# Experts: TensorE's work put in the order in which the passes are written

## The chip, the cores and the metric

The kernel runs on one core of one Trainium2 chip. TensorE multiplies matrices into PSUM, VectorE (DVE) and ScalarE (ACT) read PSUM and work on SBUF, GpSimd (POOL) helps with small things, SyncE (SP) issues the loads of the weights. The metric is the device time of one execution in microseconds, as the median of several runs.

## What is computed

The reference is a chain of two blocks of two layers each over 256 tokens of width 1024. The first block has an even mixer (gated delta rule and dilated attention), an odd mixer (differential attention and gated linear attention) and convolutional feed-forwards; the second has stick-breaking attention and retention, each followed by a mixture of experts. The change touches the mixture of experts alone, which runs once in each layer of the second block:

```python
def grouped_moe(h, router_w, router_b, w_gate, w_up, w_down):
    t = h.reshape(B * S, Dm)
    logits = t.astype(jnp.float32) @ router_w.astype(jnp.float32) + router_b.astype(jnp.float32)
    ...
    combine = jnp.sum(jax.nn.one_hot(top_idx, N_EXPERTS, dtype=jnp.float32) * top_w[..., None], axis=1)
    out = jnp.zeros(t.shape, jnp.float32)
    for e in range(N_EXPERTS):
        hidden = jax.nn.silu(t @ w_gate[e]) * (t @ w_up[e])
        out = out + combine[:, e:e + 1] * (hidden @ w_down[e]).astype(jnp.float32)
    return out.astype(h.dtype).reshape(B, S, Dm)
```

There are 16 experts, each with three matrices of 2 MB (1024 x 512 floats); a token uses two of them. 96 MB of weights are read per layer.

## The kernel before

The program is one straight line for one core. The router sorts the tokens to experts. Then `moe` works in nine passes: eight `Pair`s of experts (64 token places for each of two experts, 128 in all) and at last a `Unit`, which gives the last expert of the order 64 more places. Passes for experts that are still fuller (`more`) follow behind branches.

A pass n consists of these steps, by the names of the code:

- gather(n) (`slots`, lines 2067 to 2096): VectorE makes a selection matrix `pe`; TensorE multiplies it with the tokens (L2081, 16 matmuls of 128 columns, into the PSUM banks `ps`), and VectorE and ScalarE bring the result to `xs` (L449, L447). Two small products (L2089, L2091) give the weights `cw` and the transposed selection `pt`.
- gate(n) and up(n) (`up`, L2120): 16 matmuls each of `xs` with pieces of the expert's weights. Those of the pair's two experts alternate; expert e writes partitions 64e to 64e + 63 of the same bank. ScalarE and VectorE form silu of the gate (L728, L729), VectorE the product `h` (L2254).
- flip(n) (L2213): four transposes of `h`, copied to `hT`.
- down(n) (L2131): two halves of 512 columns, the first into the bank `pc`, the second into a bank `ps`, 8 matmuls each, again with the two experts alternating. ScalarE and VectorE weigh the result into `y` (L2099, L2100).
- scatter(n) (L2141): 8 matmuls that add `y` to the four banks of the sum.

The products of gather, gate, up and down are in 32-bit floats, and each of their matmuls shows as two records in the trace. The loop writes them interleaved over the passes: up(n), gather(n+1), scatter(n-1), flip(n), gate(n+1), down(n), and so on. But the order in the program is not that of the code. A planner sorts all instructions by what its own model of the engines says is ready, and keeps only what depends on each other in order; so it may put a matmul of gather into the middle of down. What it has put in a row, the engine then runs in that row. Two things hold an order by hand: `keep_in_program_order` for the scatters among themselves, and the helper `ordered` (line 282), which chains each instruction of an engine that is written inside it to the one before.

Weights come in pieces of 1 MB, four for each matrix of a pair: two halves of the matrix for each of two experts. SyncE asks for them (L357) in the order in which they are used: up(n), gate(n+1), down(n). They go to 20 buffers in three rings (`NW, NQ, NR = 6, 8, 6`), and a load waits until the piece that held its buffer is used up. Behind the last of them SyncE has the first weights of the next stage. The number of passes behind branches is read into a register of each engine at L2278.

Of the kernel before, what the change touches and what calls it, by code (L numbers as in the profile page):

```python
# [10 lines left out]
F32 = mybir.dt.float32  # L11
# [5 lines left out]
ALU = mybir.AluOpType  # L17
# [4 lines left out]
P = 128  # L22
S = 256
NT = S // P
D = 1024
KD = D // P
# [92 lines left out]
class Net:  # L119
# [1862 lines left out]
    def moe(self, layer, xn, out=None):  # L1982
        nc, T, tc = self.nc, self.T, self.tc
        tt, stt, ts = nc.vector.tensor_tensor, nc.vector.scalar_tensor_tensor, nc.vector.tensor_scalar
        mm = nc.tensor.matmul
        ia = 2 * layer + 1
        scale, shift = self.adac[:, ia, 8:16], self.adac[:, ia, :8]
# [4 lines left out]
        NP = N_EXP // 2  # L1992
        with self.wqs, tc.tile_pool(name=self.nm("wr"), bufs=NR) as self.wr, \
# [5 lines left out]
            def part(e, m, a):  # L1999

                d, n = dram[m], (512, 512, 256)[m]
                v = d[bass.ds(e, 1), a * n : a * n + n, :]
                return v.rearrange("o (k p) f -> p (o k) f", p=P)

            def ask(pr, m, e, a):
                nonlocal nload
                step, w = (4, 4, 2)[m], (wg, wu, wd)[m]
                if pr < 2:
                    src = w[2 * pr + e][:, a * step : a * step + step, :]
                else:  # L2010
                    src = ("dynamic", layer, m, 2 * pr + e, a)
                i = self.wload(src, [P, step, w.shape[3]],
                               ring=("wq" if nload % NB < NQ else "w" if nload % NB < NQ + NW else "wr"))
                pieces.setdefault((pr, m), []).append(i)
                nload += 1

            order = [(0, 0)]
            for pr in range(NP):
                order += [(pr, 1), *([(pr + 1, 0)] if pr < NP - 1 else []), (pr, 2)]
            def ask_all(groups):  # L2020
                for pr, m in groups:
                    for a in range(2):
                        for e in range(2):
                            ask(pr, m, e, a)
# [5 lines left out]
            def big(tag, shape, dt=F32, bufs=1):  # L2030
                if shared is not None and tag in shared:
                    return shared[tag]
                t = mp.tile(shape, dt, tag=tag, name=self.nm(tag), bufs=bufs)
                if shared is not None:
                    shared[tag] = t
                return t


            hT = big("y", [P, KD, S])
            for t in range(NT):  # L2040
                for b in range(0, KD, 4):
                    ps = self.bank()
# [5 lines left out]
            slot, comb, cnt = self.router(mp, hT)  # L2048
            io = cst["iota64"]
            acc = self.newacc()  # L2050
            extra, regs = {}, {}

            def expert_at(n, i):
                if (n, i) not in regs:
                    regs[n, i] = nc.values_load(extra[n][:1, i : i + 1], engines=[mybir.EngineType.SP],
                                                min_val=0, max_val=N_EXP - 1)
                return regs[n, i]

            def by_order():
                for i in range(4, N_EXP):  # L2060
                    for m in range(3):
                        for a in range(2):
                            self.dyn["dynamic", layer, m, i, a] = lambda i=i, m=m, a=a: part(expert_at("pxi", i), m, a)

            fin = list(cols)
# [36 lines left out]
            class Pair:  # L2102

                n = 512
# [40 lines left out]
            class Unit(Pair):  # L2145


                n = 256
# [54 lines left out]
            def gate(it, xs, ps):  # L2203
                ps = it.up(0, xs, ps)
                h = big("h", [P, 512])[:, : it.n]
                self.silu2(h, ps, h)
                return h

            def flip(h):
                n = h.shape[1]  # L2210
                ps = self.bank()
                for f in range(n // P):
                    nc.tensor.transpose(ps[:, f * P : f * P + P], h[:, f * P : f * P + P], self.ident)  # L2213
                hT = big("hT", [P, 512])[:, :n]
                self.copy(hT, ps[:, :n])
                return hT
# [21 lines left out]
                        more(u + 1)  # L2238

            its = [Pair(pr) for pr in range(NP)] + [Unit()]  # L2240
            cur = its[0].slots()
            last = self.last_expert(mp, cnt, slot, comb)
            extra.update(zip(("oh", "pxi", "x", "so", "cb"), last))
            by_order()
            ask_all(order[5:])
            h = gate(its[0], cur[0], self.cb("x"))
            back = None
            for n, it in enumerate(its):
                last = n == NP
                xs, pt, cw = cur  # L2250
                ps = it.up(1, xs, self.cb("x") if n else self.bank())
                if n == NP - 2:
                    extra["m"], extra["off"], extra["exi"] = self.extra_units(mp, extra["x"], extra["oh"])
                tt(h, h, ps, op=ALU.mult)  # L2254
                if not last:
                    cur = its[n + 1].slots()
                if n == 0:
                    for hf in range(2):
                        self.ln_fix(big("xs", [P, KD, P], bufs=2).rearrange("p (m a) c -> p m (a c)", m=2),
                                    xn, 1, layer, 0, hf * 512, 512)  # L2260
                    fin[:] = scale, shift
                if n > 0:
                    back[0].scatter(*back[1:], **({"first": True} if n == 1 else {}))
                hT = flip(h)
                if not last:
                    h = gate(its[n + 1], cur[0], self.bank())
                else:
                    tail, grow = (self.wq.tile([P, 2048], F32, tag="w", name=self.nm("tail")) for _ in range(2))
                    tail = tail.rearrange("p (t c) -> p t c", t=NT)
                    self.ada_gate_to(grow, ia)  # L2270
                back = it, pt, it.down(hT, cw)
            if out is not None:
                gb = self.wr.tile([P, 2048], F32, tag="w", name=self.nm("gb")).rearrange("p (m c) -> p m c", m=2)
                gb = [gb[:, m, :] for m in range(2)]
# [84 lines left out]
```

## Time and profile before

| | us |
|---|---|
| median of 3 runs | 1894.0 |
| lowest, highest | 1893.7, 1896.0 |
| profiled execution, its own time | 1896.7 |
| profiled execution, span from first to last instruction | 1894.7 |

| stage (us from the span's start) | from | to |
|---|---|---|
| experts of the first layer, gate(0) to the last scatter | 1072.6 | 1337.6 |
| retention, up to the experts of the second layer | 1350.5 | 1615.0 |
| experts of the second layer, gate(0) to the last scatter | 1615.0 | 1874.5 |
| last layer norm and output | 1874 | 1894.7 |

The mean granted clock of TensorE over the span is 0.959 of 2.4 GHz. A row of the timeline merges instructions of one line that follow each other: start, duration, engine, line, operation, what it writes and reads, tile, count, and in brackets the idle time before it and what ended that. "128*64" is the part of the array that a matmul uses. A row's duration holds the end of its last matmul, which overlaps the next row's start, so the length of a step is taken from start to start. A row of the windows gives the stretch and its length, the busy time (and count) of TensorE, its weight loads, VectorE, ScalarE and GpSimd, then the granted clock, the mean busy share of the 16 DMA engines and what they moved in GB/s.

### The profile page before, as it was taken

Reading aid. Unit: us, or ns where it says so; the run is one execution under the profiler, and the core shown is the slowest. Engines: PE = TensorE matmul, PEld = TensorE weight load, DVE = VectorE, ACT = ScalarE, POOL = GpSimd, SP = SyncE. Lnnn points to the kernel's source line nnn. Section 1 sums busy time; section 2 is a strip of 40 time slices with the busy share of each in tenths; the row PEclk is TensorE's granted clock in tenths of the full one; section 3 lists DMA queues with packets and bytes.
Section 4 is the critical chain, followed back from the end, with each engine's and each line's share of the span. In section 5 each row is a group of like instructions: output and inputs, shape, how many; then the busy total and the mean of one; then the engine's idle time right before and its main releaser. Section 6 shows DMA issues by size and latency. Waiting matters only on the chain. (4 is left out here: it accounts for less than half of the span.)

```text
span 1894.7 us, 29642 instructions
## 1 busy us (share of the span) xinstructions
PE 1755.2 (93%) x11781; PEld 1348.1 (71%) x11781; DVE 1042.5 (55%) x2003; ACT 711.0 (38%) x1346; POOL 229.7 (12%) x275
## 2 busy tenths in 40 slices
PE   7999998999989989999799799999689997999995
PEld 6989876999879769998798444434589975444432
DVE  6865755877767558777655532111576656422113
ACT  5344434555555445554654111101334332111111
POOL 2111101000043110000300000000133320100002
PEclk9999998999989989999899799999789998999998
DMA  8454544456566674555535899992444458899940
GB/s 271 156 167 157 172 162 158 168 187 201 182 201 210 227 241 156 200 192 183 189 118 202 327 401 399 401 394 68 141 131 154 155 207 329 309 402 399 404 173 24
DMA packets 270059, 422.30 MB, mean 223 GB/s; under 512 B 10357, under 2 KB 175815, under 8 KB 269781
## 3 DMA queue, kind: packets, MB, share of 16 engines
q1 hardware_dynamic: 266516, 415.91, 62.4%
q0 software_dynamic: 2016, 2.49, 0.5%
q8 instruction: 97, 1.59, 0.3%
q10 hardware_dynamic: 1377, 1.88, 0.3%
q14 instruction: 53, 0.43, 0.1%
HBM read 419.19 MB, written 1.05 MB: 222 GB/s over the span
## 5 line engine op out<-in xcount | busy, mean ns | idle before, releaser
L271 DVE TENSOR_TENSOR wl<-w,wh 128x1024 fp32r<-128x1024 f32 (+1 forms) x312 | 386.3, 1239 | 198.5 <-ACT wh L270 194.4
L270 ACT ACTIVATE wh<-w 128x1024 fp32r<-128x1024 f32 (+1 forms) x312 | 328.6, 1055 | 364.1 <-PE ps L404 173.0
L403 PE MATMUL ps<-xh,wh 128*128 128x256 f32 (+1 forms) x1312 | 384.4, 293 | 8.8 <-ACT xh L437 8.0
L404 PE MATMUL ps<-xl,wh 128*128 128x256 f32 (+1 forms) x1312 | 375.9, 287 | 0.0
L405 PE MATMUL ps<-xh,wl 128*128 128x256 f32 (+1 forms) x1312 | 374.9, 286 | 0.1
L403 PEld LDWEIGHTS ps<-xh,wh 128*128 128x128 f32 (+1 forms) x1312 | 252.6, 193 | 16.2 <-ACT xh L437 8.3
L404 PEld LDWEIGHTS ps<-xl,wh 128*128 128x128 f32 (+1 forms) x1312 | 252.6, 192 | 3.2 <-issue 0.8
L405 PEld LDWEIGHTS ps<-xh,wl 128*128 128x128 f32 (+1 forms) x1312 | 252.1, 192 | 2.0 <-issue 0.7
L403 PE MATMUL ps<-wh,xh 128*128 128x256 f32 x512 | 156.5, 306 | 2.5 <-DVE rvg L729 1.9
L405 PE MATMUL ps<-wh,xl 128*128 128x256 f32 x512 | 149.2, 292 | 1.0 <-DVE xl L438 1.0
L404 PE MATMUL ps<-wl,xh 128*128 128x256 f32 x512 | 149.8, 293 | 0.0
L404 PE MATMUL pc<-wl,yh 128*128 128x512 f32 x336 | 132.7, 395 | 0.0
L403 PE MATMUL pc<-wh,yh 128*128 128x512 f32 x336 | 131.7, 395 | 0.9 <-DVE yl L271 0.9
L405 PE MATMUL pc<-wh,yl 128*128 128x512 f32 x336 | 131.2, 391 | 0.3
L2120 PE MATMUL pc<-w,xs 128*64 128x512 f32 x512 | 121.6, 595 | 0.0
L2120 PE MATMUL ps<-w,xs 128*64 128x512 f32 x512 | 113.3, 595 | 0.9 <-ACT pt L265 0.9
L403 PEld LDWEIGHTS ps<-wh,xh 128*128 128x128 f32 x512 | 102.5, 200 | 6.7 <-issue 2.2
L405 PEld LDWEIGHTS ps<-wh,xl 128*128 128x128 f32 x512 | 102.1, 199 | 2.0 <-DVE xl L438 1.8
L404 PEld LDWEIGHTS ps<-wl,xh 128*128 128x128 f32 x512 | 102.7, 201 | 0.4 <-issue 0.2
L2081 PEld LDWEIGHTS ps<-pe,x 128*128 128x128 f32 x576 | 72.3, 204 | 28.1 <-issue 25.2
L2120 PEld LDWEIGHTS pc<-w,xs 128*64 128x64 f32 x512 | 37.4, 137 | 72.8 <-issue 69.8
L2131 PE MATMUL ps<-w,hT 128*64 128x512 f32 x256 | 88.5, 595 | 0.0
(573 smaller groups left out, 2633.3 us busy)
## 6 DMA issues: line engine op xcount, KB each, us to landing
w<-in_moe_w_gate_dram SPq DMA_DIRECT2D x64, 1024.0 KB, 13.2
w<-in_moe_w_up_dram SPq DMA_DIRECT2D x64, 1024.0 KB, 14.6
w<-in_moe_w_down_dram SPq DMA_DIRECT2D x64, 1024.0 KB, 14.2
w<-in_ada_w_dram SPq DMA_DIRECT2D x48, 1024.0 KB, 5.5
w<-in_ffn_w_up_dram SPq DMA_DIRECT2D x44, 1024.0 KB, 5.4
w<-in_ret_w_in_dram SPq DMA_DIRECT2D x24, 1024.0 KB, 5.2
w<-in_ffn_w_down_dram SPq DMA_DIRECT2D x22, 1024.0 KB, 5.1
w<-in_w_in_even_dram SPq DMA_DIRECT2D x21, 1024.0 KB, 5.3
```

Of the source, the lines that this page charges most:

```text
L270: self.nc.scalar.activation(hi, src, AF.Copy)
L271: self.nc.vector.tensor_tensor(lo, src, hi.bitcast(F32), op=ALU.subtract)
L403: mm(ps, lh, rh, start=first, stop=False)
L404: mm(ps, lh, rl, start=False, stop=False)
L405: mm(ps, ll, rh, start=False, stop=last)
L2081: mm(ps[:, k * P : k * P + P], xn[:, t, (4 * a + k) * P : (4 * a + k + 1) * P], pef[:, t, :], start=t == 0, stop=t == 1)
L2120: mm(ps[64 * e : 64 * e + 64, :], xs[:, k, 64 * e : 64 * e + 64], wt[2 * (k // 4) + e][:, k % 4, :], start=k == 0, stop=k == KD - 1)
L2131: mm(ps[64 * e : 64 * e + 64, :], hT[:, f * P + 64 * e : f * P + 64 * e + 64], wt[2 * (f // 2) + e][:, f % 2, hf * 512 : hf * 512 + 512], ...
```

## The change

The nine passes, from the first gather to the ninth pass, are put inside `with self.ordered(nc.tensor.engine)`. Nothing else changes; the body of the loop is the same, indented. The two reads of the router's numbers and the loads that are asked for between the passes stand inside it too, but only instructions of TensorE are chained.

```diff
             its = [Pair(pr) for pr in range(NP)] + [Unit()]
-            cur = its[0].slots()
-            last = self.last_expert(mp, cnt, slot, comb)
...
-            h = gate(its[0], cur[0], self.cb("x"))
-            back = None
-            for n, it in enumerate(its):
...
-                back = it, pt, it.down(hT, cw)
+
+            with self.ordered(nc.tensor.engine):
+                cur = its[0].slots()
+                last = self.last_expert(mp, cnt, slot, comb)
...
+                h = gate(its[0], cur[0], self.cb("x"))
+                back = None
+                for n, it in enumerate(its):
...
+                    back = it, pt, it.down(hT, cw)
```

The helper is the one that the kernel has already:

```python
    def ordered(self, *engines):
        bb = self.nc.cur_bb.bb.instructions
        n = len(bb)
        yield
        last = {}
        for i in list(bb[n:]):
            if i.engine in engines:
                if i.engine in last:
                    self.tc.add_manual_dep(i, last[i.engine], ..., reason="ordered")
                last[i.engine] = i.name
```

In the first layer the rows of TensorE differ from down(3) on, in the second from up(4) on; from there to down(7) they differ in each pass, in the same way. TensorE around down(4) of the first layer, before; `pc_12341` and `ps_12352` are the two halves of down, `w_11635` and `w_11639` pieces of one expert, `w_11637` and `w_11641` of the other, `ps_12387` and `ps_12400` the banks of gather(6):

```order
 L2131 MATMUL pc_12341<-w_11635,hT_12318 64x512
 L2131 MATMUL ps_12352<-w_11635,hT_12318 64x512
 L2081 MATMUL ps_12387<-pe_12384,x_81 128x128 x7
 L2131 MATMUL pc_12341<-w_11637,hT_12318 64x512
 L2131 MATMUL pc_12341<-w_11635,hT_12318 64x512
 L2131 MATMUL pc_12341<-w_11637,hT_12318 64x512
 L2131 MATMUL ps_12352<-w_11637,hT_12318 64x512
 L2131 MATMUL ps_12352<-w_11635,hT_12318 64x512
 L2131 MATMUL ps_12352<-w_11637,hT_12318 64x512
 L2081 MATMUL ps_12387<-pe_12384,x_81 128x128
 L2081 MATMUL ps_12400<-pe_12384,x_81 128x128 x5
```

The same place after the change:

```order
 L2131 MATMUL pc_12341<-w_11635,hT_12318 64x512
 L2131 MATMUL pc_12341<-w_11637,hT_12318 64x512
 L2131 MATMUL pc_12341<-w_11635,hT_12318 64x512
 L2131 MATMUL pc_12341<-w_11637,hT_12318 64x512
 L2131 MATMUL pc_12341<-w_11639,hT_12318 64x512
 L2131 MATMUL pc_12341<-w_11641,hT_12318 64x512
 L2131 MATMUL pc_12341<-w_11639,hT_12318 64x512
 L2131 MATMUL pc_12341<-w_11641,hT_12318 64x512
 L2131 MATMUL ps_12352<-w_11635,hT_12318 64x512
 L2131 MATMUL ps_12352<-w_11637,hT_12318 64x512
```

The first half of down now stands whole ahead of the second, the experts alternate from row to row, and gather(6) has moved behind up(5), where it stands whole ahead of scatter(4).

VectorE's rows follow. From the gate's part of `h` to `hT` of pass 5 in the first layer, before:

```order
 L729 SCALAR_TENSOR_TENSOR h_12337<-h_12337,ps_12320 128x512
 L449 TENSOR_SCALAR xs_12381<-ps_12387,adac 128x128 x2
 L449 TENSOR_SCALAR xs_12381<-ps_12400,adac 128x128
 L2074 TENSOR_TENSOR pe_12533<-cst_9764,upso_11456 128x128 x2
 L449 TENSOR_SCALAR xs_12381<-ps_12400,adac 128x128
 L2100 SCALAR_TENSOR_TENSOR y_12340<-pc_12341,cw_12151,y_12340 128x512
 L2100 SCALAR_TENSOR_TENSOR y_12340<-ps_12352,cw_12151,y_12340 128x512
 L2094 TENSOR_SCALAR cw_12383<-ps_12413 64x1 x2
 L2254 TENSOR_TENSOR h_12337<-h_12337,pc_12363 128x512
 L267 COPY hT_12434<-ps_12429 128x512
```

And after:

```order
 L729 SCALAR_TENSOR_TENSOR h_12337<-h_12337,ps_12320 128x512
 L2100 SCALAR_TENSOR_TENSOR y_12340<-pc_12341,cw_12151,y_12340 128x512
 L2100 SCALAR_TENSOR_TENSOR y_12340<-ps_12352,cw_12151,y_12340 128x512
 L2256 TENSOR_TENSOR h_12337<-h_12337,pc_12363 128x512
 L449 TENSOR_SCALAR xs_12381<-ps_12387,adac 128x128 x2
 L449 TENSOR_SCALAR xs_12381<-ps_12400,adac 128x128
 L2094 TENSOR_SCALAR cw_12383<-ps_12413 64x1 x2
 L2074 TENSOR_TENSOR pe_12533<-cst_9764,upso_11456 128x128 x2
 L449 TENSOR_SCALAR xs_12381<-ps_12400,adac 128x128
 L267 COPY hT_12434<-ps_12429 128x512
```

The weighing of down (L2100) and the product `h` (L2254, now L2256) have moved ahead of what belongs to gather; ScalarE's rows move alike.

SyncE at the end of the first layer's experts, as a difference; `uexi_12520` holds the numbers behind the branches, `w_...` are buffers of the next stage's weights:

```order
 L357 DMA w_11749<-in_ret_w_in_dram 128x8x256
+L2280 TENSOR_LOAD uexi_12520
+L2280 ISA x2
 L357 DMA w_11751<-in_ret_w_in_dram 128x8x256
 L357 DMA w_11753<-in_ret_w_in_dram 128x8x256
 L357 DMA w_11755<-in_ret_w_in_dram 128x8x256
-L2278 TENSOR_LOAD uexi_12520
-L2278 ISA x2
```

The read of the register has moved ahead of three loads. SyncE's loads of the experts' weights keep their order.

## Rows read from the trace of the kernel before

**Rows 1.** The page: the engines' busy time, and a group of down.

```profile
PE 1755.2 (93%) x11781; PEld 1348.1 (71%) x11781; DVE 1042.5 (55%) x2003; ACT 711.0 (38%) x1346; POOL 229.7 (12%) x275
...
L2131 PE MATMUL ps<-w,hT 128*64 128x512 f32 x256 | 88.5, 595 | 0.0
```

**Rows 2.** Windows: first layer, stretches 3 and 6; second layer, stretch 6.

```profile
1146.68:1174.12 27.44, 27.44 (x147) 12.92 (x146) 6.01 (x13) 4.19 (x8) 0.00 (x0) 1.00 1.04 399
1242.96:1277.57 34.61, 33.71 (x148) 13.89 (x147) 5.92 (x13) 4.19 (x8) 0.00 (x0) 1.00 1.03 399
1779.88:1814.49 34.61, 33.72 (x148) 13.89 (x147) 5.92 (x13) 4.18 (x8) 0.00 (x0) 1.00 1.04 397
```

**Rows 3.** Timeline of TensorE, first layer, stretch 3 and the start of 4.

```profile
1146.68 7.09 PE L2120 MATMUL ps<-w,xs 128*64 128x512 f32 x32
1153.60 3.60 PE L2131 MATMUL pc<-w,hT 128*64 128x512 f32 x16
...
1160.46 7.04 PE L2120 MATMUL pc<-w,xs 128*64 128x512 f32 x32
1167.43 3.84 PE L2081 MATMUL ps<-pe,x 128*128 128x128 f32 x32
...
1171.64 2.12 PE L2141 MATMUL pc<-y,pt 128*128 128x512 f32 x8
...
1174.12 7.09 PE L2120 MATMUL ps<-w,xs 128*64 128x512 f32 x32
```

**Rows 4.** Timeline of TensorE, first layer, stretch 6 and the start of 7.

```profile
1249.88 1.02 PE L2131 MATMUL pc<-w,hT 128*64 128x512 f32 x2
...
1265.48 1.35 PE L2141 MATMUL pc<-y,pt 128*128 128x512 f32 x3
...
1276.98 0.66 PE L2213 MATMUL ps<-ident,h 128*128 128x128 f32 x4 [0.78 <-DVE h L2254]
1277.57 7.09 PE L2120 MATMUL ps<-w,xs 128*64 128x512 f32 x32
```

**Rows 5.** SyncE's loads of down(7): durations, first and last issue; issue to landing.

```profile
L357 SPq DMA_DIRECT2D w<-in_moe_w_down_dram x4: 373/704/2358, 1258.6 to 1265.6; - x4
...
DMA to landing us min/median/max: 12.6/13.4/14.2
...
L357 SPq DMA_DIRECT2D w<-in_moe_w_down_dram x4: 1030/1074/2349, 1800.5 to 1805.7; - x4
...
DMA to landing us min/median/max: 13.8/14.5/17.5
```

**Rows 6.** Windows of 10 us, from both layers' stages.

```profile
1100.00:1110.00 10.00, 10.00 (x50) 3.43 (x48) 4.69 (x5) 1.37 (x2) 2.66 (x4) 1.00 1.05 384
...
1280.00:1290.00 10.00, 10.00 (x49) 4.28 (x46) 0.69 (x1) 0.60 (x1) 0.00 (x0) 1.00 0.00 0
...
1340.00:1350.00 10.00, 0.00 (x0) 0.00 (x0) 8.54 (x16) 0.38 (x1) 2.41 (x6) 0.53 0.00 1
...
1620.00:1630.00 10.00, 10.00 (x51) 3.82 (x48) 1.37 (x2) 0.60 (x1) 0.44 (x1) 1.00 0.98 367
```

**Rows 7.** Timeline of TensorE: gate(8) and up(8), gate(4), gate(8) and up(8).

```profile
1312.17 3.67 PE L2178 MATMUL ps<-w,xs 128*64 128x256 f32 x32
...
1323.49 3.67 PE L2178 MATMUL pc<-w,xs 128*64 128x256 f32 x32 [0.72 <-DVE y L2100]
...
1716.63 7.09 PE L2120 MATMUL ps<-w,xs 128*64 128x512 f32 x32
...
1849.09 3.67 PE L2178 MATMUL ps<-w,xs 128*64 128x256 f32 x32
...
1860.41 3.67 PE L2178 MATMUL pc<-w,xs 128*64 128x256 f32 x32 [0.72 <-DVE y L2100]
```

**Rows 8.** Reads of the count at L2278 by GpSimd and by SyncE.

```profile
L2278 POOLq TENSOR_LOAD <-uexi x2: 302/396/491, 1106.1 to 1820.8; - x2
L2278 SPq TENSOR_LOAD <-uexi x2: 267/402/536, 1327.6 to 1809.5; - x2
```

More of the change, by code (lines that the diff above doesn't have):

```diff
@@ L2240, in moe @@
             its = [Pair(pr) for pr in range(NP)] + [Unit()]
-            cur = its[0].slots()
-            last = self.last_expert(mp, cnt, slot, comb)
-            extra.update(zip(("oh", "pxi", "x", "so", "cb"), last))
-            by_order()
-            ask_all(order[5:])
-            h = gate(its[0], cur[0], self.cb("x"))
-            back = None
-            for n, it in enumerate(its):
[L2249 to L2270, printed above, removed]
-                back = it, pt, it.down(hT, cw)
@@ new lines, in moe @@
+            with self.ordered(nc.tensor.engine):
+                cur = its[0].slots()
+                last = self.last_expert(mp, cnt, slot, comb)
+                extra.update(zip(("oh", "pxi", "x", "so", "cb"), last))
+                by_order()
+                ask_all(order[5:])
+                h = gate(its[0], cur[0], self.cb("x"))
+                back = None
+                for n, it in enumerate(its):
+                    last = n == NP
+                    xs, pt, cw = cur
+                    ps = it.up(1, xs, self.cb("x") if n else self.bank())
+                    if n == NP - 2:
+                        extra["m"], extra["off"], extra["exi"] = self.extra_units(mp, extra["x"], extra["oh"])
+                    tt(h, h, ps, op=ALU.mult)
+                    if not last:
+                        cur = its[n + 1].slots()
+                    if n == 0:
+                        for hf in range(2):
+                            self.ln_fix(big("xs", [P, KD, P], bufs=2).rearrange("p (m a) c -> p m (a c)", m=2),
+                                        xn, 1, layer, 0, hf * 512, 512)
+                        fin[:] = scale, shift
+                    if n > 0:
+                        back[0].scatter(*back[1:], **({"first": True} if n == 1 else {}))
+                    hT = flip(h)
+                    if not last:
+                        h = gate(its[n + 1], cur[0], self.bank())
+                    else:
+                        tail, grow = (self.wq.tile([P, 2048], F32, tag="w", name=self.nm("tail")) for _ in range(2))
+                        tail = tail.rearrange("p (t c) -> p t c", t=NT)
+                        self.ada_gate_to(grow, ia)
+                    back = it, pt, it.down(hT, cw)
```

## The prediction

> **What bounds the kernel now.** I read the page first, then the busy time by stretches, then the timeline of the places that the change reorders. TensorE is busy for 93% of the span [rows 1], so what counts is how long its work takes, stage by stage. I count the expert stage in stretches, each from the first matmul of gate(n) to that of gate(n+1): gate(n), down(n-1), up(n), gather(n+1), scatter(n-1), flip(n). A stretch holds the same 147 or 148 matmul records wherever it stands, yet stretch 3 of the first layer takes 27.44 us and stretch 6 takes 34.61, and so does stretch 6 of the second layer. Clock (1.00), DMA rate (397 to 399 GB/s), VectorE's and ScalarE's busy time are alike, and TensorE counts as busy for nearly all of each [rows 2]. So the reader is to see that busy time says nothing here: the slow stretches do the same work in another order.
>
> The timeline of the two shows where the time is. In stretch 3 (written order) the steps follow one another without an idle row: gate 6.92 us (1146.68 to 1153.60), down 6.86, up 6.97, gather 4.21, scatter and flip 2.48 [rows 3]. In stretch 6 the gate takes the same 6.92, but down and gather, mixed, take 15.60 (1249.88 to 1265.48) where the written order takes 6.86 + 4.21 = 11.07: 4.53 more. Scatter mixed with the first matmuls of up, the rest of up, an idle 0.78 and flip take 12.09 (1265.48 to 1277.57) where 6.97 + 2.48 = 9.45 do: 2.64 more, of which 0.78 is TensorE waiting for VectorE's product h [rows 4]. Together 7.17, which is the whole difference. The reason stands in the expert products: in written order their matmuls alternate between the two experts, which sit in different halves of the array (128*64), and 16 records take 3.43 us, 0.21 each (half of down's 6.86). Out of that order two records of one half follow each other: the pair at 1249.88 takes 1.02, where one alone has a mean of 0.59, so the second starts 0.43 behind the first [rows 1, 4].
>
> What might bound the stage instead is the weights' transfer: 12 MB in 12 pieces per stretch, at the DMA engines' full share (1.04) and 399 GB/s [rows 2], that is 12.58 MB / 0.399 = 31.5 us. That is above 27.45 and below 34.61. But the transfers end early: the last four pieces of the first layer are issued by 1265.6 and take at most 14.2 to land, so all is there by 1279.8, and in the second layer by 1805.7 + 17.5 = 1823.2 [rows 5]; from 1280 on no bytes move [rows 6], while up(8) starts at 1323.49 and 1860.41 [rows 7]. TensorE is the one that is late, by its own order.
>
> **The change, part by part.** It adds no work; it fixes TensorE's order. By the listing of the program, stretches 1 to 3 already stand as written, and the change rewrites stretches 4 to 7 and down(7) in each layer (in the second layer's stretch 4 only two matmuls of gather leave up).
>
> (1) Stretches 4 to 7. In the first layer they run from 1174.12 [rows 3] to 1312.17 [rows 7], 138.05 us. In written order each should take what stretch 3 does, 27.45: 109.80 in all, 28.25 less. Second layer: 1716.63 to 1849.09 [rows 7], 132.46, less 109.80: 22.66. I take 27.45 because after the change the rows of VectorE and ScalarE in these stretches follow the same sequence as those of stretches 2 and 3 do now, so what TensorE waits for comes equally early. The idle 0.78 goes too: in written order gather and scatter (4.21 us and most of 2.48) stand between up and flip, h is formed meanwhile, and stretch 3 has no idle row there [rows 3]; were that cover gone, 0.8 per stretch would come back, 6 in all.
>
> (2) gate(8) and down(7). From gate(8) to up(8) it is 11.32 now (1312.17 to 1323.49, 1849.09 to 1860.41 [rows 7]), with 0.72 idle on VectorE's y. gate(8) is half a gate, 3.5, and down in written order 6.86: 10.36, 0.96 less in each layer, 1.9 in all. The bank that up(8) needs is then read out while the second half of down runs (3.43 us), so no wait is left.
>
> (3) VectorE's and ScalarE's new order costs nothing: they are busy 5.9 and 4.2 us of 34.61 [rows 2].
>
> (4) In the first layer SyncE's read of the expert count (L2278) moves ahead of three loads of the next stage's weights. It takes 0.27 to 0.54 us, and the number has long been there: GpSimd reads it at 1106.1 [rows 8]. Queued behind it on SyncE are the three loads, which wait for buffers that TensorE frees later; were all three late by their whole transfer (3.15 MB at 0.399, 7.9 us), TensorE would be idle there anyway, for the whole of 1340 to 1350 [rows 6]. I take zero, and 0.5 as its upper end.
>
> (5) The weights. A piece can be asked for when its buffer is free: 20 buffers, so each group of four waits for the group five before it, which TensorE finishes earlier than now. Landings are then at least as early as now. But TensorE consumes a stretch in 27.45 and DMA brings it in 31.5, so its lead falls by 4.0 us a stretch and is tightest at up(7). First layer: gate(7) would start at 1174.12 + 3 x 27.45 = 1256.47, up(7) at +6.92 + 6.86 = 1270.25, its second half at 1273.7. up(7)'s weights are the group before the last: 1279.8 less the last group's 4.19 MB / 0.399 = 10.5 gives 1269.3, 4.4 us ahead. Second layer: up(7)'s second half at 1716.63 + 82.35 + 13.78 + 3.48 = 1816.2, its last piece at 1823.2 - 10.5 = 1812.7, 3.5 ahead. down(7) has 7.6 and 6.7. So no wait by these rows. Were the rate that of the slowest 10 us nearby, 384 [rows 6], over the 95 us from 1174 to 1269 (38 MB), the landing would be 3.8 later, in time in the first layer and some tenths late in the second; at 367 (the stretch in which the second layer's transfers restart [rows 6]) it would be 8.3 later, a wait of 4 to 5 per layer.
>
> The Trainium skill speaks against the change here: "DMA: Bandwidth & Descriptors", section Specifications, gives an HBM limit of about 358 GB/s per core. By that limit the 38 MB would take 106 us, up(7) would wait some 7 us in each layer, and the sum would come out at about 1855 (an estimate from that page's figure). The rows hold 397 to 399 GB/s, so here the measurement decides [rows 2].
>
> **The sum.** 28.25 + 22.66 + 1.92 = 52.8 us. What follows (layer norms, next stage, the chain at the end) depends on TensorE's end and shifts as a whole. The profiled execution took 1896.7 (span 1894.7), which gives 1843.9; it lies 2.7 above the median of 1894.0, so against the median 1894.0 - 52.8 = 1841.2, about **1841**. Its own bounds: 1838.5, if the runs of after lie as far under this as the profiled one of before lies over its median; 6 more, if waits of 0.8 stay in each stretch.
>
> **The rivals.**
> A, the weights come late at the end: the lead of 3.5 to 4.4 us is used up at up(7) and a wait of 4 to 5 per layer takes the place of the disorder: 1841 + 9 = 1850. For: the margin is a few per cent of what is moved since 1174. Against: DMA's share is full in every stretch now, and the buffers come free earlier, not later. Chance 0.09.
> B, DMA sets the pace of every changed stretch from the start: 31.5 instead of 27.45, gaining 3.1 in each of the seven stretches of about 34.6 (the second layer's stretch 4 takes 132.46 - 3 x 34.61 = 28.6 as it is): 1894 - 22 = 1872. For: 31.5 is what 12 pieces take. Against: stretches 2 and 3 already run at 27.45 with the same 399 GB/s, and gate(4)'s weights, twelve groups before the last, are there by 1279.8 - 12 x 10.5 = 1153.8, 20 us ahead of its start. Chance 0.04.
> C, slower: TensorE waits for weights in the last stretches, the clock falls, and it runs at 1.2 GHz instead of 2.4. Where TensorE is idle between 1340 and 1350, the granted clock is 0.53 [rows 6]. A stretch at half clock would take 54.9; two of them give 54.9 back, more than the gain, and four (the last two in each layer) end at 1841 + 4 x 27.45 = 1951. Against: (5) finds no wait at all, and the 0.78 of idle in stretch 6 leave the clock at 1.00 [rows 2, 4]. Chance 0.03.
> D, the change doesn't do what it says (the planner keeps mixing): the listing shows the written order in both layers, so 0.01 at 1894, and 0.01 for anything else without effect.
>
> **How the numbers follow.** Forecast 0.82, A 0.09, B 0.04, C 0.03, D 0.02. The forecast with its bounds runs from 1838.5 to 1847; with most of A the range is 1838 to 1850. 0.2% (3.8 us) is about what a measurement of this kernel can tell from no change; the forecast, A and B are beyond it on the fast side: faster 0.95, same 0.02, slower 0.03.
>
> **What would show it.** In the profile after: stretches 4 to 7 of both layers at 27.4 to 27.5 with gate, down, up, gather, scatter, flip as single rows; no idle before flip; up(8) at about 1294 and, 29 us earlier than now to begin with, 1808; the retention stage between as long as before; DMA still ending near 1280 in the first layer, now only some 14 us ahead of up(8)'s start. An idle row in front of up(7), or gate(7), with a DMA as its releaser means A; stretches of 31 us mean B; a granted clock under 1.00 inside the stage means C. The forecast is wrong if a stretch in written order late in the stage takes longer than the early ones for a reason that no row of before shows.

## The result, and the profile after

The changed kernel takes 1842.6 us (median of 4 runs, 1841.3 to 1843.2), the kernel before, run beside it, 1894.2 (4 runs): a ratio of 0.9725 with a 95% interval of 0.9708 to 0.9742, 51.6 us less. The forecast was 1841, in a range of 1838 to 1850. The profiled execution took 1843.2 (span 1841.1).

The page of the changed kernel, the rows that answer to [rows 1]:

```profile
PE 1707.9 (93%) x11781; PEld 1338.1 (73%) x11781; DVE 1043.0 (57%) x2003; ACT 711.6 (39%) x1346; POOL 230.9 (13%) x275
...
L2131 PE MATMUL ps<-w,hT 128*64 128x512 f32 x256 | 57.6, 592 | 0.0
```

TensorE is busy for the same 93% with the same 11781 instructions. What shrank is busy time, by 47.3 us. The group of down has the same mean duration as before (592 ns against 595) but a busy time of 57.6 us instead of 88.5: its 256 records, some 152 us if laid end to end, now lie more closely over one another. The mean of one record told nothing either time.

Windows of stretch 6, first and second layer, the answer to [rows 2]:

```profile
1230.20:1257.66 27.46, 27.46 (x147) 12.92 (x147) 6.01 (x13) 4.19 (x8) 0.00 (x0) 1.00 1.04 402
...
1741.44:1768.89 27.45, 27.45 (x147) 12.92 (x146) 6.01 (x13) 4.19 (x8) 0.00 (x0) 1.00 1.04 402
```

Both took 34.61 before. All seven stretches of each layer now take 27.45. The timeline of TensorE in the first layer's stretch 6, to be laid beside [rows 3, 4], and then gate(8), up(8) and the next stage's first matmul:

```profile
1230.21 7.09 PE L2120 MATMUL ps<-w,xs 128*64 128x512 f32 x32
1237.12 3.60 PE L2131 MATMUL pc<-w,hT 128*64 128x512 f32 x16
1240.56 3.60 PE L2131 MATMUL ps<-w,hT 128*64 128x512 f32 x16
1243.99 7.04 PE L2120 MATMUL pc<-w,xs 128*64 128x512 f32 x32
1250.96 3.84 PE L2081 MATMUL ps<-pe,x 128*128 128x128 f32 x32
...
1255.17 2.12 PE L2141 MATMUL pc<-y,pt 128*128 128x512 f32 x8
1257.13 0.60 PE L2213 MATMUL ps<-ident,h 128*128 128x128 f32 x4
...
1285.11 3.67 PE L2178 MATMUL ps<-w,xs 128*64 128x256 f32 x32
...
1295.48 3.62 PE L2178 MATMUL pc<-w,xs 128*64 128x256 f32 x32
...
1323.33 2.82 PE L424 MATMUL ps<-ident,x 128*128 128x128 f32 x12 [13.80 <-ACT x L708]
```

Each step is one row again, the wait ahead of the flip is gone, and so is the one at up(8) [rows 7]. From gate(4) to up(8) the first layer takes 120.18 us (149.37 before), the second 120.19 (143.78): 29.19 and 23.59 less, 52.78 together, where the prediction had 29.21 and 23.62.

### The profile page after: what moved, and what is told of

The parts are those of the page before. It is cut to its first block, busy times and chain, and to the rows that moved or that the text cites. A ratio compares the mean times of both kernels' runs of the same rounds, so it can differ in the third digit from the quotient of the medians.

```text
span 1841.1 us, 29655 instructions
## 1 busy us (share of the span) xinstructions
PE 1707.9 (93%) x11781; PEld 1338.1 (73%) x11781; DVE 1043.0 (57%) x2003; ACT 711.6 (39%) x1346; POOL 230.9 (13%) x275
## 3 DMA queue, kind: packets, MB, share of 16 engines
q10 hardware_dynamic: 1377, 1.88, 0.3%
HBM read 419.19 MB, written 1.05 MB: 228 GB/s over the span
## 5 line engine op out<-in xcount | busy, mean ns | idle before, releaser
L2120 PE MATMUL pc<-w,xs 128*64 128x512 f32 x512 | 112.7, 592 | 0.0
L2120 PEld LDWEIGHTS ps<-w,xs 128*64 128x64 f32 x512 | 35.5, 137 | 68.5 <-issue 67.1
L722 DVE SCALAR_TENSOR_TENSOR ffy<-ps,ffcw,ffy 128x255 f32<-128x255 f32 (+1 forms) x176 | 84.1, 478 | 1.5
```

What stands on the lines that cost most here:

```text
L722: nc.vector.scalar_tensor_tensor(out[:, sft:], ps[:, : S - sft], w(width - 1 - sft), out[:, sft:], op0=ALU.mult, op1=ALU.add)
L2120: mm(ps[64 * e : 64 * e + 64, :], xs[:, k, 64 * e : 64 * e + 64], wt[2 * (k // 4) + e][:, k % 4, :], start=k == 0, stop=k == KD - 1)
```

## Experiments

Each run edits the changed kernel, but for e1, which puts a part of the change into the kernel before. "Stretch" is the distance from one gate to the next, read from the timeline. The first four runs set the prediction's reason (a record that follows one of its own half of the array costs 0.43) against others, and try the layers apart; the reason did not stand. Of the later seven, six test what took its place, and e7 the margin of the weights.

**e1, down alone kept in order.** The kernel before, with the written order for the 16 matmuls of down (the lines of down below stand indented inside it, otherwise as they were):

```diff
+                    with self.ordered(nc.tensor.engine):
                     for hf in range(2):
                         ps = self.cb("x") if hf == 0 else self.bank()
```

> The kernel before, with the order fixed inside down alone (16 matmuls of one pass chained); everything else is left to the planner. In its listing down stands whole with the experts alternating, and gather now breaks into up in three places, so that four of up's 16 matmuls stand next to none of the other half. Theory (what costs is that two matmuls of one half of the array follow each other): in stretches 4 to 7 four matmuls at 0.86 instead of 0.43 us, 1.7 more than the written order's 27.45, and up to 0.5 for the changes of shape, so 29.2 to 29.7 per stretch; 1856 to 1861 us in all. Rival (what costs is gather's 128-column matmuls among the 64-column ones, wherever they stand): the 4.5 us that mixing costs per stretch stay, 1875 to 1880.

Measured: 1862.7 us, ratio 0.985 (0.981 to 0.988); the mixed stretches take 30.18. Neither expectation was met; the theory came nearer. In the timeline of e1, down is whole again, and up is cut by pieces of gather instead, as the listing had it:

```profile
1181.13 3.60 PE L2132 MATMUL pc<-w,hT 128*64 128x512 f32 x16
1184.56 3.60 PE L2132 MATMUL ps<-w,hT 128*64 128x512 f32 x16
1187.99 1.02 PE L2120 MATMUL pc<-w,xs 128*64 128x512 f32 x2
1188.94 1.38 PE L2081 MATMUL ps<-pe,x 128*128 128x128 f32 x10
1190.26 3.65 PE L2120 MATMUL pc<-w,xs 128*64 128x512 f32 x14
1193.84 0.71 PE L2081 MATMUL ps<-pe,x 128*128 128x128 f32 x4
```

A matmul is two records here. The one matmul at 1187.99 takes 0.95 us to the next row, and the seven behind it 3.58, not 7 x 0.43 = 3.0. Inside the piece of seven the two experts alternate. Seven is odd: four matmuls of one expert, three of the other, and 4 x 0.86 = 3.44.

**e2, one half after the other.** The changed kernel with all four matmuls of expert 0 ahead of those of expert 1, in each half of down's output:

```diff
-                        for f in range(4):
-                            for e in range(2):
+                        for e in range(2):
+                            for f in range(4):
```

> The changed kernel, with its strict order, but in down the loops over experts and over the 128-row blocks are exchanged: four matmuls of one half of the array, then four of the other. Nothing is mixed into down. Theory of the halves: down takes up to twice its 6.86 us, less the three places in which the half changes (0.43 each), so 5.6 to 6.9 more in each of 16 downs: 1932 to 1953 us. Rival (the disorder costs through gather, scatter or the banks that come between): no change, 1843.

Measured: 1872.6 us, ratio 0.989 (0.985 to 0.993), stretches of 29.33: 1.88 more than in order, in each of the seven. The prediction's reason asked for 5.6 to 6.9 (up to 32 records at 0.43 in place of 6.87 us), its rival for nothing; both missed. Two views of e2's timeline, the start of a down product and a place within it:

```profile
1159.38 1.88 PE L2131 MATMUL pc<-w,hT 128*64 128x512 f32 x4
...
1163.30 0.59 PE L2131 MATMUL pc<-w,hT 128*64 128x512 f32 x1
1163.36 0.59 PE L2131 MATMUL ps<-w,hT 128*64 128x512 f32 x1
1163.73 0.59 PE L2131 MATMUL pc<-w,hT 128*64 128x512 f32 x1
1163.79 0.59 PE L2131 MATMUL ps<-w,hT 128*64 128x512 f32 x1
```

Four records run alone, 0.43 apart; then the halves run side by side although the program has eight records of one ahead of the first of the other. At 1163 TensorE works on pc in one half and already on ps, written later, in the other. So each half has work waiting of its own, and what is lost is the four records (4 x 0.43 = 1.72) during which the second half had nothing yet. That fits a queue of some three records behind the running one, which is an inference from this run alone. The Trainium skill, "TensorE: Matmul & The Clock Gate", section "Part 3: Packing small matmuls — row/col tiling", holds that matmuls start and end strictly in program order. These rows show records written later starting ahead of earlier ones, so here the measurement decides. The rows also narrow what was said of the kernel before, that the engine runs the planner's row in that row: in e2 the two halves of the array do not keep the row between them.

**e3, down's two banks in turn.** The changed kernel with the output halves taken in turn, the experts still alternating:

```diff
-                    for hf in range(2):
-                        for f in range(4):
-                            for e in range(2):
+                    for hf, f in ((0, 0), (1, 0), (0, 1), (0, 2), (1, 1), (0, 3), (1, 2), (1, 3)):
+                        for e in range(2):
```

> The changed kernel, with down's two banks taken in turn (blocks 0 | 0 | 1 2 | 1 | 3 | 2 3 of the first, second, first ... half of the columns) and the experts still alternating from matmul to matmul. The planner's order before had both: banks in turn, and halves of the array out of turn. Theory of the halves: down stays at 6.9 us, and only the later weighing of the first bank may hold up the next up by some tenths, 1842 to 1847 us. Rival (the change of bank costs, five changes per down): about as much as the mixing cost, 4.5 us in each of 16 downs, 1915.

Measured: 1859.2 us, ratio 0.982 (0.978 to 0.986), outside both, and nearer the theory's 1842 to 1847 than the rival's 1915. Six of the seven stretches take 27.59, as the theory had them (0.14 more than in order). The rest is in the first stretch of each layer, 34.24 and 34.90. There, in the timeline of e3, TensorE and then VectorE; the window of up's start (of TensorE alone: length, busy time, clock, DMA share, GB/s); and VectorE's row in the changed kernel:

```profile
1110.84 9.65 PE L2120 MATMUL pc<-w,xs 128*64 128x512 f32 x32 [4.01 <-DVE y L2100]
```

```profile
1107.24 2.88 DVE L614 TENSOR_TENSOR x<-x,xs 128x1024 f32<-128x1024 f32 x2 [5.69 <-POOL xs L609]
1110.04 0.75 DVE L2100 SCALAR_TENSOR_TENSOR y<-pc,cw,y 128x512 fp32r<-128x512 f32 x1
```

```profile
1110.84:1116.00 5.16, 5.16 (x12) 0.50 1.05 385
```

```profile
1104.58 0.75 DVE L2100 SCALAR_TENSOR_TENSOR y<-pc,cw,y 128x512 fp32r<-128x512 f32 x1 [2.75 <-ACT y L2099]
```

up needs the bank pc, which VectorE empties at L2100. In the changed kernel's timeline pc is finished 3.4 us ahead of ps and read at 1104.58, before L614 at 1107.59; here it comes behind L614, which waits for GpSimd. The wait is 4.01 of the 6.79 us that this stretch loses. Most of the rest is the clock: behind the wait TensorE is granted 0.50 until 1116, the lower of its two levels, and up takes 9.59 us to the next row (1110.84 to 1120.43) where it takes 6.97 at full clock. So the banks cost next to nothing on TensorE (0.14), and this edit broke a cover that only the first stretch needs.

**e4, the written order in the first layer alone.**

```diff
-            with self.ordered(nc.tensor.engine):
+            with self.ordered(*([nc.tensor.engine] if layer == 0 else [])):
```

> The order is fixed in the first layer's experts alone; the second layer's are those of the kernel before. Theory (the gain of a layer shifts all that follows by as much): 28.25 + 0.96 = 29.2 us under the kernel before, 1865. Rival (part of the first layer's gain is given back in the retention stage, whose first weights are asked for while the last experts' weights still come in): 1870 or more, with a longer idle time of TensorE ahead of the retention stage.

Measured: 1865.4 us, ratio 0.986 (0.982 to 0.989). First layer: all stretches 27.45; second: 28.65, 34.60, 34.61, 34.60 from stretch 4 on, as before. As far as runs that spread over 3 us tell, the layers' gains add (1842.6 + 23.6 = 1866.2), and neither gives anything back to the other.

**The theory after these four**, so far an argument. Each half of the array works through its own short queue, so order alone costs little. But the matmuls of gather, scatter and flip use the whole array (128*128 in the rows): they wait until both halves are empty, and the halves wait for them. Between two such barriers a piece takes 0.86 us times the larger of the two experts' counts of matmuls, in place of 0.43 times their sum; and each further change between half and whole costs something by itself. The next runs take order, cuts and uneven pieces apart, in four passes of each layer (stretches 4 to 7).

**e5, the old order of down, no cuts.**

```diff
+                    if 3 <= s.pr <= 6:
+                        pss = [self.cb("x"), self.bank()]
+                        for g in (0, 2):
+                            for hf, f, e in ((0, g, 0), (1, g, 0), (0, g, 1), (0, g + 1, 0),
+                                             (0, g + 1, 1), (1, g, 1), (1, g + 1, 0), (1, g + 1, 1)):
+                                mm(pss[hf][64 * e : ...
```

> The changed kernel, but in four passes of each layer (those whose down product was mixed with a gather in the kernel before) the 16 matmuls of down stand in the order they had there, the two output banks in turn and the two experts out of turn, with no gather between them. Theory (barrier): each half of the array works off a short queue of its own, so that an order out of turn costs next to nothing unless a matmul that needs the whole array stands behind it; the four stretches take 27.5 to 27.9 us and the kernel 1843 to 1847 us. Rival (out of turn costs by itself): in this order four matmuls of the sixteen follow one on the same half, which at 0.86 us each is 3.4 us per stretch: stretches of 30.9 us and a kernel of about 1870 us.

Measured: 1848.1 us, ratio 0.975 (0.973 to 0.977), stretches of 28.45, half a microsecond over the theory's bound of 27.9 and far under the rival's 30.9. Timeline of e5 at the next up:

```profile
1191.18 7.09 PE L2120 MATMUL pc<-w,xs 128*64 128x512 f32 x32 [0.73 <-DVE y L2100]
```

0.73 of the 1.00 is up's wait for the bank, as in e3; the order itself costs 0.27.

**e6, the gather cut into down, even pieces.** The gather made a generator that down advances by 7, 6 and 3 matmuls, as many as before, but always behind a pair of both experts (the buffers of `cw` go from 2 to 3 for it):

```diff
+                            for _ in range({(0, 1): 7, (0, 3): 6, (1, 1): 99}.get((hf, f), 0)):
+                                next(step, None)
```

> The changed kernel, but in the same four passes of each layer the gather of the pass after next is cut into the down product, in three pieces of 7, 6 and 3 matmuls as in the kernel before; the matmuls of down keep the written order, so that each piece of down between two pieces of the gather holds as many matmuls of one expert as of the other. Theory (barrier): what costs is the number of one expert's matmuls beyond the other's between two barriers, here none; what is left is three more changes of shape at about 0.33 us, stretches of 28.4 to 28.6 us, a kernel of 1850 to 1852 us. Rival (the cutting itself costs, whatever stands in the pieces): down and gather take the 15.6 us they took in the kernel before in place of 11.1, stretches of about 32 us, a kernel of 1878 to 1881 us.

Measured: 1848.4 us, ratio 0.975 (0.974 to 0.977). The stretches take 28.49, 1.04 more for three more changes between half and whole, 0.35 each; the total came out some 2 us under what was expected, by parts outside the stretches. Timeline of e6:

```profile
1182.42 1.89 PE L2140 MATMUL pc<-w,hT 128*64 128x512 f32 x8
1184.24 1.83 PE L2089 MATMUL ps<-pe,x 128*128 128x128 f32 x14
```

Four matmuls of down, two of each expert, take 1.82 between their start and the gather's. The Trainium skill, "TensorEngine Tiling (Array Packing)", section "Key Properties", says that a change of the tiling mode drains TensorE; it gives no price, and these rows give one.

With 0.35 for a change the count also gives e1's stretch. Between its pieces of gather, up stands in pieces of 1, 7, 1 and 7 matmuls, so (1 + 4 + 1 + 4) x 0.86 in place of 8 x 0.86, 1.72 more, and three more changes at 0.35: 27.45 + 1.72 + 1.05 = 30.22 us a stretch, against 30.18 measured.

**e8, both together.** The old order and the cuts at their old places, so that the pieces hold 2 matmuls of one expert and none of the other, 2 and 4, 2 and 0, 2 and 4. Within e5's loop:

```diff
+                                for _ in range({(0, 1): 7, (0, 7): 6, (2, 1): 99}.get((g, i), 0)):
+                                    next(step, None)
```

> The changed kernel with both edits of the two runs before this one together, in four passes of each layer: the down product in its old order out of turn, and the gather of the pass after next cut into it in pieces of 7, 6 and 3 matmuls at the old places. By itself the old order took 28.45 us a stretch (0.73 of it a wait of up for its bank), the cut by itself 28.49, the changed kernel 27.45. Theory (barrier): between the pieces of the gather the down product now holds 2 matmuls of one expert and none of the other, 2 and 4, 2 and 0, 2 and 4; each piece takes 0.86 us times the larger number, 10.3 us in place of 6.9; so 28.49 + 3.44 = 31.9 us a stretch, or 32.7 with the wait for the bank, and a kernel of 1877 to 1884 us. Rival (the two costs add): 27.45 + 1.00 + 1.04 = 29.5 us a stretch, a kernel of about 1857 us.

Measured: 1876.8 us, ratio 0.990 (0.987 to 0.993); stretches of 32.00 to 32.02, as the theory had them without the wait for the bank, which is gone. The order alone cost 1.00, the cuts alone 1.04, both together 4.56. This is the verdict on the reason: the costs do not add, they arise where uneven pieces meet barriers. Timeline of e8, the first piece, and the gather behind the same piece in the kernel before:

```profile
1213.62 1.02 PE L2141 MATMUL pc<-w,hT 128*64 128x512 f32 x2
1214.47 1.02 PE L2141 MATMUL ps<-w,hT 128*64 128x512 f32 x2
1215.43 1.83 PE L2089 MATMUL ps<-pe,x 128*128 128x128 f32 x14
```

```profile
1251.68 1.83 PE L2081 MATMUL ps<-pe,x 128*128 128x128 f32 x14
```

Two matmuls of one expert take 1.81 (1213.62 to 1215.43), as long as four do in e6; in the kernel before they take 1.80 (from 1249.88 [rows 4] to 1251.68).

**e9, up late; e10 and e11, the scatter cut.** In the kernel before, up stood behind the gather in these stretches, its first matmul within the scatter. e9 moves up whole to just ahead of the flip (`late` is 4 <= n <= 7). e10 and e11 also cut the scatter, by one matmul of up and by two; the two edits:

```diff
+                    if late:
+                        ps = it.up(1, xs, self.cb("x"))
+                        tt(h, h, ps, op=ALU.mult)
                     hT = flip(h)
```

```diff
+                        back[0].scatter(*back[1:], hi=3)
+                        ps = it.up(1, xs, self.cb("x"), 1, lambda: back[0].scatter(*back[1:], lo=3))
```

> The changed kernel, but in the passes 4 to 7 of each layer the up product stands whole behind the gather and the scatter, just ahead of the flip, as the last 15 of its 16 matmuls did in the kernel before. Nothing is cut and nothing is out of turn. Theory: the flip now waits for VectorE's product of up and h, 0.78 us as in the kernel before, and there is one more change of shape at about 0.33 us: 28.5 to 28.7 us a stretch, a kernel of 1851 to 1853 us. Rival (the place of up costs all that the stretch's second part lost, 2.63 us): 30.1 us a stretch, about 1864 us.

> The run with up late, with its scatter cut after 3 of 8 matmuls by the first matmul of up, as the kernel before had it in those passes. Theory (barrier): up now stands in two blocks, one matmul of expert 0 alone and then 7 of expert 0 with 8 of expert 1; (1 + 8) x 0.86 = 7.73 us in place of 6.87, and one more change of shape at about 0.35 us: 28.70 + 0.86 + 0.35 = 29.9 us a stretch, a kernel of about 1862 us. Rival (every cut costs the same, whatever stands between): the same stretch as in the run whose scatter is cut by two matmuls of up.

> The same, with the scatter cut by the first two matmuls of up, one of each expert. Theory (barrier): 1 of each and 7 of each, (1 + 7) x 0.86 = 6.87 us as uncut; only the change of shape is left, 28.70 + 0.35 = 29.05 us a stretch, a kernel of about 1855 us, though one matmul more stands inside the cut than in the run beside it. Rival (every cut costs the same): the stretch of the run beside it, and where all that is still unaccounted of the kernel before (34.61 - 32.00 - 1.25 = 1.36 us) is the cut's, 30.06 us in both.

Measured: e9 1852.8 us (ratio 0.978, 0.976 to 0.980), stretches of 28.70; e10 1864.8 (0.984, 0.983 to 0.986), 29.85; e11 1857.4 (0.980, 0.978 to 0.982), 29.04. All three stretches as the theory had them; e10's and e11's medians lie 2.8 and 2.4 over what was expected. In e11's profile parts outside the stretches make the difference; e10's profile is of its fastest execution (1860.1), so no trace shows what its median holds more. Timelines of e9, e10 and e11, a row or two of each:

```profile
1233.16 0.63 PE L2213 MATMUL ps<-ident,h 128*128 128x128 f32 x4 [0.91 <-DVE h L2271]
```

```profile
1221.50 1.07 PE L2120 MATMUL pc<-w,xs 128*64 128x512 f32 x2
1222.50 1.44 PE L2145 MATMUL pc<-y,pt 128*128 128x512 f32 x5
1223.87 7.08 PE L2120 MATMUL pc<-w,xs 128*64 128x512 f32 x30
```

```profile
1224.66 1.08 PE L2120 MATMUL pc<-w,xs 128*64 128x512 f32 x4
1225.67 1.44 PE L2145 MATMUL pc<-y,pt 128*128 128x512 f32 x5
1227.03 6.23 PE L2120 MATMUL pc<-w,xs 128*64 128x512 f32 x28
```

e10 beside e11 is the plainest reading: between the two parts of the scatter one matmul alone takes 1.00 us and two, one of each expert, 1.01. The second is free, and the 15 left over in e10 take 0.85 more than the 14 in e11.

**e7, is there a margin of the weights?** The changed kernel without the gather matmuls of the passes 5 to 8:

```diff
+                old = shared is None and kept["n"] > 5
+                xs, pt = kept["xs"] if old else big("xs", [P, KD, P], bufs=bufs), big("pt", [P, S], F32R, bufs=3)
...
-                for a in range(2):
+                for a in range(0 if old else 2):
```

> The changed kernel without the 16 gather matmuls of the passes 5 to 8 and the copies behind them (these passes take the gathered inputs of an earlier pass again, so the output is another); TensorE's work per stretch falls by 3.65 us, to 23.8, in the stretches 4 to 7. Theory (the weights are next): the pieces of up(7) land when they landed, since SyncE's queue moved its bytes without a pause, so TensorE uses up the margin of some 4 us and then waits at up(7) or just ahead of it; a layer gains about 4 + 3.65 us (the gather behind up(7)), the kernel 15 to 17 us: 1826 to 1828. Rival (the loads come sooner when the buffers come free sooner): no wait, four times 3.65 us in each layer, 1813 to 1814 us.

Measured: 1823.4 us, ratio 0.963 (0.961 to 0.965). Stretches 4 to 6 take 23.88; stretch 7 takes 30.27 in the first layer and 30.54 in the second. Timeline of e7, first layer, stretch 7:

```profile
1253.25 1.07 PE L2135 MATMUL pc<-w,hT 128*64 128x512 f32 x2 [0.63 <-DMA w<-in_moe_w_down_dram]
1255.82 1.50 PE L2135 MATMUL pc<-w,hT 128*64 128x512 f32 x5 [1.50 <-DMA w<-in_moe_w_down_dram]
...
1266.62 3.65 PE L2124 MATMUL pc<-w,xs 128*64 128x512 f32 x14 [1.62 <-DMA w<-in_moe_w_up_dram]
```

TensorE waits for weights at down(6) and in up(7); from gate(4) to gate(8) the layers gain 7.89 and 7.64 of the 4 x 3.57 = 14.3 that were taken out, where the theory had 4 + 3.65 and its rival all of it. The first layer's stretch 7 is 6.39 longer than its stretch 6; the idle rows hold 3.75 of that. The total is 3 us under the expected one; in e7's profile the expert stage starts 3.9 earlier than in that of the changed kernel (1069.8 against 1073.7), ahead of any edit.

## Why the prediction was right

**Stretches 4 to 7**: predicted 28.25 and 22.66 less, measured 28.24 and 22.64 (109.81 and 109.82 us from gate(4) to gate(8)). The step held because it took the written order's price from rows of the same kernel ([rows 3]) instead of building it up from a mechanism.

**The reason behind it was wrong in its general form.** "Two records of one half follow each other, so the second starts 0.43 behind the first" is true of the pair at 1249.88 [rows 4], but that pair stands before a gather. Where none follows, the second half of the array catches up: e5 has the same order and pays 0.27 plus a wait. That this did no harm to the forecast is owed to the step above, which does not use the reason. What the runs put in its place, for the 7.16 us of a stretch (34.61 - 27.45): down and gather 4.56 (e8: 1.04 for the cuts by e6, 3.44 by the count of uneven pieces, under 0.1 left), up late 1.25 (e9: 0.91 of it the wait for h, the rest a change of shape), the scatter's cut 0.34 (e11) and its uneven pieces 0.81 (e10 less e11). That is 6.96; 0.2 stay open, and no run joins the two parts, so the sum rests on their adding up. The prediction's split, 4.53 and 2.64, agrees with 4.56 and 2.40. What gather and scatter share in the rows is that they use the whole array; that this is what makes them a barrier is the reading, for no run gave one of them half an array.

**gate(8) and down(7)**: 10.37 from gate(8) to up(8) (1285.11 to 1295.48), no idle row; predicted 10.36.

**The weights**: TensorE's matmuls wait for no load in the stage, as predicted, at 386 to 405 GB/s over stretches 4 to 7 of the first layer, so rivals A and B fell. All that they wait for in either layer's stage, in the view of waits of the changed kernel (line, releaser, us in total, times, longest):

```profile
PE pc L2199 <- PEq L2220: 1.2, 1, 1.2
PE ps L2120 <- ACT pt L265: 0.5, 1, 0.5
```

The 358 GB/s of the Trainium skill ("DMA: Bandwidth & Descriptors", Specifications), by which the estimate was 1855, are no limit in these rows. The margin at up(7) was put at 4.4 and 3.5 us. In the second layer the changed kernel's trace shows the last piece of up(7) from issue to landing:

```profile
L357 SPq DMA_DIRECT2D w<-in_moe_w_up_dram x1: 2295/2295/2295, 1768.1 to 1768.1; - x1
...
DMA to landing us min/median/max: 13.8/13.8/13.8
```

It lands at 1781.9 and is needed halfway through up(7) (1782.68 to 1789.64), at 1786.1: 4.2. In the first layer this landing is not in the trace, but e7 gives an estimate: there the last piece of up(7) releases TensorE at 1266.62, 95.21 after gate(4). At the same distance the changed kernel would have it at 1175.30 + 95.21 = 1270.5, and needs it halfway through up(7) (1271.44 to 1278.41), at 1274.9: 4.4 again. The last piece of the first layer lands at 1281.6 (issued at 1264.9, 16.7 before), 13.9 ahead of up(8), where 14 was foreseen. Counted from gate(4) that is 106.3, and 105.7 before [rows 5]: "at least as early" was off by 0.6.

**The clock** stays at 1.00 in stretches 4 to 7, so rival C fell. A fall of the kind that C feared did show in e3, where 0.50 followed on 4.01 us without a matmul, there for a bank and not for weights; e7's waits of 0.63 to 1.62 us left the clock at 1.00 (windows from 1243.05 to 1273.33). SyncE's earlier read of the count shows in no wait: TensorE's next start is released by ScalarE's x at L708, as part of the layer norm.

**The sum**: 52.8 predicted, 51.6 by the medians and 53.6 by the two spans. The 52.78 inside the stages are common to both; what differs lies outside. In the profile after, gate(4) of the first layer starts 1.2 later, the idle ahead of the retention stage is 0.9 longer (13.80 after 12.89; 12.1 to 13.5 in the experiments), and the retention stage is 2.9 shorter (261.6 against 264.5 up to the second layer's first gate). "As long as before" was thus a miss for that stage; over the eleven experiments it took 258.6 to 263.1. With a single profile of the kernel before, whether its 264.5 is chance or an effect of the order stays open. That these parts nearly cancel, and that the median came out 1.6 from the forecast of 1841, is in part luck.

## What to carry to other kernels

When small matmuls share the array and others use the whole of it, keep the shared ones together, and if they must be cut, cut where every part of the array has had equally many. The same matmuls in an order out of turn cost little by themselves (e5: 0.27 us, and 0.73 of waiting for a bank) until something that needs the whole array stands among them (e8). Price a reordering from a stretch of the same kernel that already runs in the new order, then ask how far the weights are ahead: here some 4 us are left, and e7 shows that what is saved beyond them turns into waiting.

## What was not expected of the hardware

- The halves of the array run ahead of one another: with eight records of one half first, only four ran alone (e2), 1.88 us a stretch where strict order would have cost up to 6.9 (an estimate: 32 records 0.43 apart).
- A change between half and whole array, there and back, costs about 0.35 us (e6 1.04 for three, e11 0.34 for one).
- One matmul alone between two whole-array ones takes 1.00 us, a pair of both experts 1.01 (e10, e11).
